# Splitting the second layer's weights in a background stream during the first layer of a two-layer mixer trunk

## The chip, the cores and the metric

The kernel runs on one core of one Trainium2 chip. The metric is the device time of one execution in microseconds. Before the change it is 2655.73 us, the median of 3 runs (2654.89 to 2658.55).

## The reference

A sequence of 2048 tokens of width 1024 passes through two layers. Each layer normalises and modulates its input, projects it once to all heads, runs gated linear attention on one half and differential softmax attention on the other, gates both, and projects back. All inputs are 32-bit floats.

```python
for l in range(DEPTH):                                   # 2 layers
    shift, scale, gate = jnp.split(c_act @ w_ada[l] + b_ada[l], 3, axis=-1)
    h = rms_norm(x, norm_g[l]) * (1.0 + scale[:, None]) + shift[:, None]
    gq, gk, gv, glr, gz, dq, dk, dv, dz = split_columns(h @ w_in[l])
    gqkv = jax.nn.silu(causal_depthwise_conv(jnp.concatenate([gq, gk, gv], axis=-1), conv_w[l]))
    o_gla = gla_branch(*split3(gqkv), glr, gz, w_gk[l], b_gk[l], gla_norm_g[l])
    o_diff = diff_branch(dq, dk, dv, dz, qn_g[l], kn_g[l], lam, lam_init, diff_norm_g[l])
    x = x + gate[:, None] * (jnp.concatenate([o_gla, o_diff], axis=-1) @ w_out[l])
```

## The kernel before, in words

Each layer works through the sequence in four blocks of 512 tokens (`u` = 0 to 3). The dense projections are made of three matmuls for each product: the activations and the weights are each split into a high part of a shorter format and a low part (the rest), and high x high, high x low and low x high are added up. A weight matrix is nine items: four attention heads (items 0 to 3), two pieces of the convolved group (4 and 5), the gate (6) and the two halves of the output projection (7 and 8). Each item has eight weight tiles, one for each 128 rows, so a layer has 72. A tile `w` holds both parts, 128 x 2 x 512, and feeds 12 matmuls of 128x512.

`weights` (L552) delivers such a tile. In a layer's first block (`u` = 0) it loads the raw weights into a tile `raw` (three buffers), casts them to the high part on ScalarE, subtracts on GpSimd for the low part, and writes the tile to DRAM (`wd`). In the three later blocks it reads the kept tile back from `wd`. The tiles `w` come from the pool `p_w` with four buffers (L301).

`dense_gen` (L1013) runs the projections of a block, `out_gen` (L1064) its output projection. `head_evac` (L836) takes a head's result out of PSUM: ScalarE copies queries and keys into a tile `rw` of 128x256 (four buffers), squares are summed, GpSimd takes the power, and VectorE writes the normalised values to a tile `qk`, which TensorE then transposes. `conv_evac` (L674) does the convolution: ScalarE copies a bank into `ub`, VectorE runs four taps into a tile `t` and makes `uT`, with a tanh on ScalarE between. `prep_gen` (L605) makes the input of the next block. The attention writes scores and probabilities in tiles `s`, their transposes in `aT`.

The order of the instructions is decided in two steps. `run_streams` (L518) steps through generators (dense, attention, linear attention, preparation and others), each of which yields estimates of TensorE time or names an event it needs, and records their operations in one list. `Program.order` (L188) then schedules that list: with an estimated duration for each operation it fills each engine, and where several operations are ready on an engine the one recorded first goes first. Buffers of a pool are handed out in the order of recording, so an operation that needs a buffer also waits for the turn of those recorded ahead of it. Each engine and the DMA queue of SyncE (SP) then run their instructions strictly in that order. Every operation is issued from line 284, so all profile rows carry L284 and are told apart by tile names.

Of the kernel before, what the change touches and what calls it, by code (L numbers as in the profile page):

```python
# [11 lines left out]
F32 = mybir.dt.float32  # L12
# [8 lines left out]
P = 128  # L21
D = 1024
KT = D // P
# [264 lines left out]
def trunk_kernel(ctx, tc, x, c, w_ada, b_ada, norm_g, w_in, conv_w, w_gk, b_gk, gla_norm_g,  # L288
# [9 lines left out]
    p_h = pool("p_h", 1)  # L298
    p_x = pool("p_x", 1)
    p_raw = pool("p_raw", 3)  # L300
    p_w = pool("p_w", 4)  # L301
    p_oT = pool("p_oT", 8)
    p_s = pool("p_s", 4)
    p_at = pool("p_at", 3)
# [204 lines left out]
    def done(*ev):  # L509
        events[ev] = clock[0]  # L510

    def need(*ev, lag=0.0):
        return ("need", ev, lag)

    def pe(cost, wait=0.0):
        return ("pe", cost, wait)
# [35 lines left out]
    def weights(l, u, item, k, src, n=None):  # L552
        w = p_w.tile([P, 2, 512], F32R, tag="w", name="w")
        hi, lo = w[:, 0, :], w[:, 1, :]
        kept = WD[l][item][k]
        if u > 0:
            SY.dma_start(w.bitcast(F32), kept)
            return hi, lo
        raw = p_raw.tile([P, 512], F32, tag="raw", name="raw")
        SY.dma_start(raw if n is None else raw.rearrange("p (g n) -> p g n", n=n), src)  # L560
        A.copy(hi, raw)
        G.tensor_tensor(lo, raw, hi.bitcast(F32), op=ALU.subtract)
        if NU > 1:
            SY.dma_start(kept, w.bitcast(F32))
        return hi, lo

    def silu2(dst, ps, shape=(P, 512)):
        th = t2(shape)
# [267 lines left out]
    def head_evac(l, u, hd, banks):  # L836
        key = l * NU + u
        ss = p_sm.tile([P, TT, 4], F32, tag="qss", name="qss", bufs=2)
        rq = p_sm.tile([P, TT, 4], F32, tag="rq", name="rq", bufs=2)
        sz = p_z.tile([P, TT, P], F32, tag="z", name="z")  # L840
        Vt = p_kv.tile([P, TT, P], F32, tag="V", name="Vt")
        qk = []
        for t in range(TT):
            rw = p_t.tile([P, 256], F32, tag="rw", name="rw", bufs=4)
            A.copy(rw, banks[t][:, 0:256])
            th = p_t.tile([P, P], F32, tag="th", name="th", bufs=2)
            A.activation(th, banks[t][:, 384:512], AF.Tanh, scale=0.5)
            V.scalar_tensor_tensor(sz[:, t, :], th, 1.0, banks[t][:, 384:512], op0=ALU.add, op1=ALU.mult)
            A.copy(Vt[:, t, :], banks[t][:, 256:384])
            sq = p_t.tile([P, 256], F32, tag="sq", name="sq", bufs=2)  # L850
            A.activation(sq, rw, AF.Square)
            V.tensor_reduce(ss[:, t, :], sq.rearrange("p (a n) -> p a n", a=4), axis=AX.X, op=ALU.add)
            V.tensor_scalar(ss[:, t, :], ss[:, t, :], 1.0 / 64, EPS, op0=ALU.mult, op1=ALU.add)
            G.tensor_tensor(rq[:, t, :], ss[:, t, :], mhalf[:, 0:4], op=ALU.pow)
            n = p_q.tile([P, 256], F32, tag="qk", name="qk", bufs=4)
            V.tensor_tensor(n.rearrange("p (a n) -> p a n", a=4), rw.rearrange("p (a n) -> p a n", a=4),
                            rq[:, t, :].unsqueeze(2).to_broadcast([P, 4, 64]), op=ALU.mult)
            qk.append(n)
        HD[key, hd] = (qk, Vt, sz)

    def qk_gen(l, u, hd):
# [150 lines left out]

    def dense_gen(l, u, items):  # L1013
        key = l * NU + u
        yield need("h", key, lag=2.0)
        def gla_proj(grp):
            banks = []
            yield from proj_T(l, u, 4 + grp, C_GQ + 512 * grp, banks)
            if grp == 0:
                yield need("gate", key)  # L1020
            else:
                yield need("ktr", key)
            GL[f"cv{grp}"] = conv_evac(l, u, grp, banks)
            done("conv", key, grp)

        def head_proj(hd):
            def ld(k):
                src = w_in[l, k * P:(k + 1) * P, C_D:C_D + 2048].rearrange("p (g n) -> p g n", n=512)
                return weights(l, u, hd, k, src[:, :, hd * P:hd * P + P], n=P)

            banks = []
            yield from proj_N(ld, banks)
            if hd == LAST:
                done("free_h", key + 1)
            if hd >= 1:
                yield need("qkT", key, hd - 1)
            if hd >= 2:
                yield need("attn", key, hd - 2)
            head_evac(l, u, hd, banks)
            done("hev", key, hd)  # L1040

        def gate_proj():
            banks = []
            yield from proj_N(lambda k: weights(l, u, 6, k, w_in[l, k * P:(k + 1) * P, C_GZ:C_GZ + 512]), banks)
            if LAST == 4:
                done("free_h", key + 1)
            yield need("scan", key)
            osb = GL["osb"]
            for t in range(TT):
                sz = t2()  # L1050
                silu2(sz, banks[t])
                G.tensor_tensor(osb[:, t, :], osb[:, t, :], sz, op=ALU.mult)
            done("gz", key)

        LAST = 4
        for it in items:
            if it < 4:
                yield from head_proj(it)
            elif it < 6:
                yield from gla_proj(it - 4)  # L1060
            else:
                yield from gate_proj()
# [43 lines left out]
    def attn_stream():  # L1106
        for l in range(L):
            for u in range(NU):
                for hd in range(4):
                    yield from attn_gen(l, u, hd)  # L1110

    def qk_stream():
        for l in range(L):
            for u in range(NU):
                for hd in range(4):
                    yield from qk_gen(l, u, hd)

    def gla_stream():
        for l in range(L):
            for u in range(NU):  # L1120
                yield from gla_gen(l, u)

    def prep_stream():
        for l in range(L):
            for u in range(NU):
                if l > 0:
                    yield need("x", (l - 1) * NU + u)
                if l or u:
                    yield from prep_gen(l, u, io(l)[0])

    def dense_stream():
# [8 lines left out]
                prev = (l, u)  # L1140
        yield from out_gen(*prev)

    def ada_stream():
        yield need("h", 0)
        yield need("conv", 0, 1)
        yield from ada_part(0, 2, 0.0)
        for l in range(1, L):
            yield need("h", (l - 1) * NU + max(NU - 3, 0))
            yield from ada_part(l, 0, 4.0)
            yield from ada_part(l, 1, 4.0)  # L1150
            yield need("gate", l * NU - 1)
            gate_weights(l)
            yield need("x", l * NU - 1)
            yield from ada_part(l, 2, 1.0)
# [3 lines left out]
    small_vectors(False)  # L1158
    more_vectors()
    gate_weights(0)  # L1160
    run_streams([qk_stream(), attn_stream(), gla_stream(), prep_stream(), ada_stream(), dense_stream()])
    with tc.manual_schedule():
        prog.issue()

# [24 lines left out]
```

## Time and profile before

| | |
|---|---|
| Median of the runs | 2655.73 us (2654.89 to 2658.55) |
| Profiled execution | 2658.48 us |
| Its span | 2656.8 us |
| Mean granted clock of TensorE | 0.995 |
| DMA, mean over the span | 179 GB/s, 476.12 MB |

Durations in the prediction come from the profiled execution. The view by stages gives, for each stretch, the busy time of TensorE, its weight load, VectorE, ScalarE and GpSimd with the number of instructions, then the granted clock, the mean busy share of the 16 DMA engines and GB/s. The first layer's four blocks end at about 345, 655, 985 and 1362 us, and the second layer's first at about 1660 us. Rows of waits read: who waited, in front of the arrow, and for whom, behind it, then us in total, times and the longest.

### The profile page before, as it was taken

What the parts mean: (1) busy time and instruction counts of PE and PEld (TensorE: products, weight loads), DVE (VectorE), ACT (ScalarE), POOL (GpSimd) and SP (SyncE); (2) the same over time, 40 slices, a digit from 0 to 9 for tenths busy, and PEclk for the clock granted to TensorE, in tenths of its full rate; (3) what the DMA queues carried; (4) which work ended last, traced back from release to release, by engine and by line L of the source; (5) the groups of instructions that cost most, each with busy time, mean ns of one, the idle gap of its engine ahead of it and who ended that gap; (6) DMA issues with size and microseconds to landing.
All of it is one profiled execution on the core that took longest, in us unless ns stands there. A gap on an engine that the chain in (4) does not pass through costs nothing. (4 is left out here: it accounts for less than half of the span.)

```text
span 2656.8 us, 41105 instructions
## 1 busy us (share of the span) xinstructions
PE 2563.9 (97%) x13987; PEld 2066.8 (78%) x13987; DVE 1767.1 (67%) x5104; ACT 1206.7 (45%) x2592; POOL 626.2 (24%) x852
## 2 busy tenths in 40 slices
PE   7999899999999999999999989999999999999997
PEld 4777678877888778888777767887788877888886
DVE  4778757874767837776838764667637786387764
ACT  3555524443344533444734563344614456154442
POOL 2455411131010210102144554111121111210111
PEclk9999999999999999999999999999999999999999
DMA  8676586446552455433277756453374433734242
GB/s 281 237 233 238 202 296 202 155 153 216 177 184 98 151 203 175 139 131 133 87 257 254 234 203 241 166 176 135 127 265 147 154 128 116 265 124 150 92 139 103
DMA packets 201612, 476.12 MB, mean 179 GB/s; under 512 B 20734, under 2 KB 78268, under 8 KB 201404
## 3 DMA queue, kind: packets, MB, share of 16 engines
q1 hardware_dynamic: 201404, 473.50, 52.1%
q8 instruction: 111, 1.82, 0.3%
q14 instruction: 97, 0.79, 0.1%
HBM read 362.29 MB, written 111.15 MB: 178 GB/s over the span
## 5 line engine op out<-in xcount | busy, mean ns | idle before, releaser
L284 PE MATMUL acc<-w,hhi 128*128 128x512 f32 x2560 | 842.1, 404 | 6.5 <-DMA w<-wd 2.8
L284 PEld LDWEIGHTS acc<-w,hhi 128*128 128x128 f32 x2560 | 462.3, 189 | 106.0 <-issue 13.2
L284 PE MATMUL acc<-w,hlo 128*128 128x512 f32 x1280 | 506.3, 397 | 0.0
L284 ACT ACTIVATE s<-s,mx 128x512 f32<-128x512 f32 (+15 forms) x256 | 308.1, 1204 | 339.6 <-DVE s L284 337.9
L284 PE MATMUL acc<-hhi,w 128*128 128x512 f32 x1024 | 370.5, 403 | 1.2 <-DVE z L284 0.5
L284 PE MATMUL acc<-w,oh 128*128 128x512 f32 x1024 | 333.8, 401 | 8.9 <-DVE t L284 5.0
L284 DVE TENSOR_SCALAR_CACHE_REDUCE s<-sc,mx 64x64 f32<-64x64 f32 (+5 forms) x640 | 307.4, 485 | 42.9 <-PE sc L284 24.7
L284 PEld LDWEIGHTS acc<-w,hlo 128*128 128x128 f32 x1280 | 241.2, 188 | 49.9 <-issue 2.0
L284 POOL MEMSET s<- 64x64 f32 x256 | 39.3, 155 | 1020.6 <-DVE s L284 466.2
L284 POOL TENSOR_TENSOR w<-raw,w 128x512 fp32r<-128x512 f32 x144 | 195.1, 1365 | 198.2 <-ACT w L284 152.7
L284 PEld LDWEIGHTS acc<-w,oh 128*128 128x128 f32 x1024 | 189.9, 189 | 54.4 <-DVE t L284 9.4
L284 PEld LDWEIGHTS acc<-hhi,w 128*128 128x128 f32 x1024 | 192.3, 188 | 39.3 <-issue 1.2
L284 ACT COPY aT<-tp 128x512 f32<-128x512 f32 (+2 forms) x320 | 162.7, 521 | 114.4 <-PE tp L284 110.6
L284 PE MATMUL po<-Vj,aT 128*128 128x128 f32 x1536 | 205.4, 278 | 5.1 <-ACT aT L284 4.8
L284 PE MATMUL acc<-w,ol 128*128 128x512 f32 x512 | 202.7, 400 | 1.0 <-DVE ol L284 0.7
L284 PEld LDWEIGHTS po<-Vj,aT 128*128 128x128 f32 x1536 | 191.7, 193 | 14.8 <-ACT aT L284 9.5
L284 DVE SCALAR_TENSOR_TENSOR s<-s,r 128x512 f32<-128x512 f32 (+2 forms) x320 | 200.5, 676 | 2.9
L284 DVE TENSOR_SCALAR_CACHE_REDUCE s<-sc 128x512 f32<-128x512 f32 (+4 forms) x256 | 158.5, 623 | 65.2 <-PE sc L284 61.1
L284 PE MATMUL acc<-hlo,w 128*128 128x512 f32 x512 | 201.2, 393 | 0.0
L284 DVE TENSOR_TENSOR ol<-oT,oh 128x512 fp32r<-128x512 f32 x128 | 105.6, 832 | 119.1 <-ACT oh L284 108.0
L284 PE MATMUL tp<-ident,s 128*128 128x128 f32 x1088 | 172.2, 274 | 11.8 <-DVE s L284 9.4
L284 POOL TENSOR_TENSOR rq<-qss,mhalf 128x4 f32<-128x4 f32 x128 | 129.0, 1027 | 191.4 <-DVE qss L284 191.0
(167 smaller groups left out, 4204.4 us busy)
## 6 DMA issues: line engine op xcount, KB each, us to landing
w<-wd SPq DMA_DIRECT2D x432, 512.0 KB, 3.7
wd<-w SPq DMA_DIRECT2D x144, 512.0 KB, 3.2
raw<-in_w_in_dram SPq DMA_DIRECT2D x112, 256.0 KB, 4.0
Kj<-kd SPq DMA_DIRECT2D x48, 512.0 KB, 4.9
wr<-in_w_ada_dram SPq DMA_DIRECT2D x128, 128.0 KB, 2.8
kd<-Kt SPq DMA_DIRECT2D x24, 512.0 KB, 3.0
Vj<-vd SPq DMA_DIRECT2D x48, 256.0 KB, 4.1
xt<-in_x_dram SPq DMA_DIRECT2D x16, 512.0 KB, 4.0
```

What stands on the lines that cost most here:

```text
L284: getattr(self.engines[e], method)(*[real(a) for a in args], **{k: real(v) for k, v in kw.items()})
```

## The change

The first block of the second layer no longer splits its weights. A new stream, `split_stream`, does it during the first layer: after an event of the first block (`conv`, 0, 1) it takes the items 0, 4, 1, 5, 2, 3, 6, 7, 8 of the second layer and calls `split_ahead` for each, which loads, casts, subtracts and writes the same tiles as `weights` did. Between two tiles it lets 12.5 us of estimated TensorE time pass. In the second layer every block reads the kept tiles, and its first block needs the nine `split` events first. The pool `p_w` has five buffers instead of four. `head_evac` normalises `rw` in place, and the tile `qk` (four buffers of 128x256) is gone.

```diff
-    p_w = pool("p_w", 4)
+    p_w = pool("p_w", 5)
...
         kept = WD[l][item][k]
-        if u > 0:
+        if u + l > 0:
             SY.dma_start(w.bitcast(F32), kept)
             return hi, lo
...
+    def source(l, item, k):
+        rows = slice(k * P, (k + 1) * P)
+        if item < 4:
+            return w_in[l, rows, C_D:C_D + 2048].rearrange("p (g n) -> p g n", n=512)[:, :, item * P:item * P + P]
+        if item < 7:
+            col = (C_GQ, C_GQ + 512, C_GZ)[item - 4]
+            return w_in[l, rows, col:col + 512]
+        return w_out[l, rows, 512 * (item - 7):512 * (item - 6)]
+
+    def split_ahead(l, item):
+        for k in range(KT):
+            w = p_w.tile([P, 2, 512], F32R, tag="w", name="w")
+            raw = p_raw.tile([P, 512], F32, tag="raw", name="raw")
+            SY.dma_start(raw if item >= 4 else raw.rearrange("p (g n) -> p g n", n=P), source(l, item, k))
+            A.copy(w[:, 0, :], raw)
+            G.tensor_tensor(w[:, 1, :], raw, w[:, 0, :].bitcast(F32), op=ALU.subtract)
+            SY.dma_start(WD[l][item][k], w.bitcast(F32))
+            yield pe(0, 12.5)
+        done("split", l, item)
...
-            n = p_q.tile([P, 256], F32, tag="qk", name="qk", bufs=4)
-            V.tensor_tensor(n.rearrange("p (a n) -> p a n", a=4), rw.rearrange("p (a n) -> p a n", a=4),
-                            rq[:, t, :].unsqueeze(2).to_broadcast([P, 4, 64]), op=ALU.mult)
-            qk.append(n)
+            rv = rw.rearrange("p (a n) -> p a n", a=4)
+            V.tensor_tensor(rv, rv, rq[:, t, :].unsqueeze(2).to_broadcast([P, 4, 64]), op=ALU.mult)
+            qk.append(rw)
...
+        for item in range(9):
+            if l and not u:
+                yield need("split", l, item)
         yield need("h", key, lag=2.0)
...
+    def split_stream():
+        for l in range(1, L):
+            yield need("conv", (l - 1) * NU, 1)
+            for item in (0, 4, 1, 5, 2, 3, 6, 7, 8):
+                yield from split_ahead(l, item)
...
-    run_streams([qk_stream(), attn_stream(), gla_stream(), prep_stream(), ada_stream(), dense_stream()])
+    run_streams([qk_stream(), attn_stream(), gla_stream(), prep_stream(), ada_stream(), split_stream(),
+                 dense_stream()])
```

The change puts the casts and writes into other places of the order. Counted between the ends of the output projections, the 72 splits of the second layer stand in the first layer's four blocks with 14, 23, 25 and 10. The rows that follow are instructions in their order, with buffer numbers in the names.

The first place is ScalarE in layer 0's second block, in the convolution. First before, then with the change.

```order
L284 COPY aT_4358<-tp_4332 128x256
L284 ACTIVATE junk_4375,oss_4376<-po_4335 128x128
L284 ACTIVATE t2_4399<-t2_4338 128x512
L284 COPY ub_4402<-acc_4023 128x512
L284 ACTIVATE t2_4439<-t2_4397 128x512
L284 ACTIVATE s_4250,ls_4463<-s_4250,mx_4425 128x1024
```
```order
L284 ACTIVATE junk_4478,oss_4479<-po_4447 128x128
L284 ACTIVATE t2_4514<-t2_4463 128x512
L284 COPY ub_4517<-acc_4119 128x512
L284 CAST w_4543<-raw_4159 128x512
L284 ACTIVATE t2_4554<-t2_4511 128x512
L284 ACTIVATE s_4377,ls_4594<-s_4377,mx_4540 128x1024
```

A cast of a second-layer weight now stands between the last copy out of PSUM and the tanh (`t2`) and exponential (`s`) behind it.

The second place is ScalarE in layer 1's first block, behind the first head's copies. First before, then with the change.

```order
L284 ACTIVATE sq_14345<-rw_14333 128x256
L284 CAST w_14352<-raw_14249 128x512
L284 CAST w_14358<-raw_14275 128x512
L284 CAST w_14374<-raw_14307 128x512
L284 ACTIVATE qh_14407<-tp_14399,G1_599 64x512 x2
L284 CAST w_14433<-raw_14391 128x512
L284 CAST Kt_14439<-tp_14426 64x512 x2
L284 CAST w_14457<-raw_14404 128x512
L284 ACTIVATE s_13670,ls_14472<-s_13670,mx_14460 128x128
```
```order
L284 ACTIVATE sq_14734<-rw_14723 128x256
L284 ACTIVATE qh_14780<-tp_14774,G1_599 64x512 x2
L284 CAST Kt_14804<-tp_14797 64x512 x2
L284 ACTIVATE s_14106,ls_14835<-s_14106,mx_14826 128x128
L284 ACTIVATE s_14258,ls_14835<-s_14258,mx_14837 128x128
```

The five weight casts between the head's copies, the query and key casts (`qh`, `Kt`) and the first exponentials are gone.

The third place is the DMA queue of SP in layer 0's second block, around the write of that block's first keys (`kd1_0`). First before, then with the change.

```order
L284 DMA kd1_0_4121<-Kt_4098 128x1024
L284 DMA wr_4127<-in_w_ada_dram 128x256
L284 DMA wr_4131<-in_w_ada_dram 128x256
L284 DMA w_4152<-wd0_1_0_1074 128x1024
L284 DMA w_4199<-wd0_1_1_1108 128x1024
```
```order
L284 DMA kd1_0_4217<-Kt_4196 128x1024
L284 DMA wr_4224<-in_w_ada_dram 128x256
L284 DMA wr_4229<-in_w_ada_dram 128x256
L284 DMA wd1_1_1_4234<-w_4212 128x1024
L284 DMA raw_4240<-in_w_in_dram 128x4x128
L284 DMA w_4245<-wd0_1_1_1104 128x1024
```

A split's write (`wd1_1_1`, of the second layer) and the next raw load now stand in front of the weight load that follows.

## The prediction

> **What bounds the kernel now.** I read the page's busy totals first, then the span cut into stages.
>
> ```profile
> span 2656.8 us, 41105 instructions
> PE 2563.9 (97%) x13987; PEld 2066.8 (78%) x13987; DVE 1767.1 (67%) x5104; ACT 1206.7 (45%) x2592; POOL 626.2 (24%) x852
> ```
>
> TensorE (PE) is busy for 2563.9 of 2656.8 us, so only 92.9 us of the span can be won without removing matmuls, and the change removes none. The question is therefore in which stage PE stands idle. The next view gives the busy time of PE, weight load, VectorE (DVE), ScalarE (ACT) and GpSimd (POOL) by stage, then the granted PE clock, the DMA share and GB/s. I cut at the ends of the output projections. The rows are the eight blocks of 512 tokens, four per layer, with a start, a joint and a tail.
>
> ```profile
> 60.00:345.00 285.00, 262.03 (x1314) 197.93 (x1312) 212.72 (x547) 150.81 (x356) 141.46 (x152) 0.99 0.69 235
> 345.00:655.00 310.00, 302.64 (x1634) 244.53 (x1635) 211.29 (x636) 129.77 (x297) 57.12 (x91) 1.00 0.58 195
> 655.00:985.00 330.00, 328.70 (x1843) 270.39 (x1842) 221.17 (x654) 151.14 (x313) 52.28 (x88) 1.00 0.47 161
> 985.00:1320.00 335.00, 332.88 (x1897) 273.56 (x1896) 237.65 (x705) 161.85 (x307) 45.72 (x77) 1.00 0.41 140
> ...
> 1362.00:1660.00 298.00, 280.60 (x1405) 219.38 (x1404) 190.38 (x514) 145.37 (x350) 151.71 (x161) 0.99 0.70 241
> 1660.00:1950.00 290.00, 284.39 (x1529) 228.08 (x1528) 183.55 (x569) 129.75 (x297) 48.24 (x84) 1.00 0.46 161
> ```
>
> Length minus PE busy is PE's idle time. It is 22.97 us in the first block of layer 0 and 17.40 us in the first block of layer 1. In the other rows it is 7.36, 1.30 and 2.12 us (layer 0, blocks 1 to 3) and 5.61 us (layer 1, block 1). So the two blocks that split weights idle most. They are also the ones at clock 0.99, and 1% of 298 us is another 3.0 us. The most that can come back in layer 1's first block is 17.4 + 3.0 = 20.4 us, or 0.77% of the span.
>
> What PE waits for in that block (us in total, times, longest):
>
> ```profile
> PE tp L284 <- DVE uT L284: 3.3, 2, 2.5
> PE tp L284 <- DVE s L284: 3.1, 5, 1.7
> PE sc L284 <- DVE xss L284: 3.0, 1, 3.0
> PE sc L284 <- DVE Kt L284: 1.8, 3, 0.8
> PE acc L284 <- DVE t L284: 1.7, 1, 1.7
> PE po L284 <- ACT aT L284: 1.3, 2, 1.0
> ```
>
> None of these is a weight tile, and the rows left out are 1.0 us or less and on DVE or ACT too. PE does not wait for the split itself. It waits for the convolution, softmax and normalising chains on DVE and ACT. The split can only matter through what it does to those two queues, and that makes the gain hard to size.
>
> **The change part by part.** The rows of the split in that block come first, then what ACT waits for there.
>
> ```profile
> L284 ACT CAST w<-raw x69: 602/620/723, 1363.7 to 1637.7; 128x512 fp32r<-128x512 f32 x69
> L284 POOL TENSOR_TENSOR w<-raw,w x69: 1266/1292/1892, 1366.8 to 1638.4; 128x512 fp32r<-128x512 f32 x69
> ```
> ```profile
> ACT w L284 <- DMA raw<-in_w_in_dram: 23.5, 13, 3.8
> ACT w L284 <- PE acc L284: 21.8, 13, 4.9
> ```
>
> *Removed from layer 1's first block.* 69 casts x 0.620 = 42.8 us leave ACT, of its 145.4. 69 subtracts x 1.292 = 89.1 us leave POOL, of 151.7. ACT also stands 23.5 + 21.8 = 45.3 us at the head of its queue with a cast that waits for its raw tile or for a free weight tile. Behind that cast stand the exponentials, the tanh of the convolution and the PSUM copies, as the rows of the order show. The subtracts on POOL also hold DVE up, as the same DVE instruction shows in this block and in layer 0's second block, which has no split (min/median/max ns):
>
> ```profile
> L284 DVE SCALAR_TENSOR_TENSOR t<-ub,vec,t x24: 737/744/1661, 1415.3 to 1490.3; 128x512 f32<-128x512 f32 x24
> ```
> ```profile
> L284 DVE SCALAR_TENSOR_TENSOR t<-ub,vec,t x24: 733/746/754, 400.4 to 519.8; 128x512 f32<-128x512 f32 x24
> ```
>
> The median is the same but the longest is 1661 against 754 ns, so single DVE steps of the convolution lose up to 0.91 us, and the wait that costs PE most in all (uT) is for the end of that convolution. The idle time of 17.4 us can stay whole (gain 0), or it can fall to the 5.61 us of the next block, which loads its weights ready (gain 11.8). The first block has the least attention work to put between dependent steps, so I do not take the whole fall. I take half of 17.4, a **gain of 8.7 us**.
>
> *The clock.* These rows are PE around its uT wait.
>
> ```profile
> 1428.19 0.39 PE L284 MATMUL acc<-w,hlo 128*128 128x512 f32 x1
> 1428.42 0.39 PE L284 MATMUL acc<-w,hhi 128*128 128x512 f32 x1
> 1431.30 1.09 PE L284 MATMUL tp<-ident,uT 128*128 128x128 f32 x4 [2.49 <-DVE uT L284]
> 1432.04 0.78 PE L284 MATMUL acc<-w,hhi 128*128 128x512 f32 x1
> ...
> 1433.90 0.63 PE L284 MATMUL acc<-w,hlo 128*128 128x512 f32 x1
> 1434.32 0.73 PE L284 MATMUL acc<-w,hhi 128*128 128x512 f32 x2
> ```
>
> Before the wait large matmuls start 0.23 us apart. After it they start 0.42 us apart until about 1434.3. A wait of 2.5 us thus costs some 1.5 us more. I return half of the block's 3.0 us with half of the waits, a **gain of 1.5** (bounds 0 and 3.0). [...]
>
> *Added to layer 0.* The order of the changed kernel has 14 splits in its first block and 23, 25 and 10 in the next three. Each brings a raw load, a cast, a subtract and a write to DRAM. Layer 1's first block reads 72 tiles of 512 KB back instead of loading raw ones. Price of a split in a first block, from the idle and clock that I ascribe to it above the level of the next block: (17.4 - 5.6 + 3.0) / 69 = 0.21 us. The 14 in layer 0's first block, where ACT (150.8 us) and POOL (141.5) already carry 72, cost 14 x 0.21 = **3.0 us** (bounds 0 and double, 6.0).
>
> The other 58 go into blocks where PE has attention work to cover with. In the two later rows, idle is only 1.30 and 2.12 us of 330 and 335. The trace has no split beside such work. The bounds are 0 and 58 x 0.21 = 12.2 us. I take a quarter, since those rows are nearest to no loss, which is **3.0 us**. The cover is the matmul queue of PE, and where it fails the full 0.21 is paid. The 58 x 0.620 = 36 us of casts go to ACT, which is busy 129.8 to 161.9 us per block there.
>
> *The fifth weight tile.* Issue and landing:
>
> ```profile
> w<-wd SPq DMA_DIRECT2D x432, 512.0 KB, 3.7
> wd<-w SPq DMA_DIRECT2D x144, 512.0 KB, 3.2
> raw<-in_w_in_dram SPq DMA_DIRECT2D x112, 256.0 KB, 4.0
> ```
>
> A weight tile feeds 12 matmuls, 12 x 0.23 = 2.8 us of PE. With four tiles a load can start three tiles (8.3 us) ahead of its use, and with five it is four (11.0 us). A split tile occupies one slot for its cast, subtract and write, at least 0.62 + 1.29 + 3.2 = 5.1 us. While it does, the stream falls back to the four of before, whose 8.3 us still covers 3.7. So I expect no new weight wait. PE's only weight wait between 345 and 1320 us is this one:
>
> ```profile
> PE acc L284 <- DMA w<-wd: 2.8, 2, 1.7
> ```
>
> It lies right behind the first block. I count a **gain of 2.0** (bounds 0 and 2.8). Split writes also stand in SP's in-order queue, waiting for POOL, with weight loads behind them. That wait is inside the same 8.3 us.
>
> *In place normalising of rw.* The multiply keeps its size and engine, so it costs 0. The cover is that the next head's copies into rw come at least one projection later, 96 matmuls or 22 us, and the transposes that free rw are done by then. If that cover went, the copy would hold PSUM banks and each microsecond would be PE's.
>
> **Sum.** -8.7 - 1.5 + 3.0 + 3.0 - 2.0 = -6.2 us. The profiled execution took 2658.48 us, of which 1.7 lie outside the span, so it becomes 2652.3. The median of the runs, 2655.73, is 2.75 us below the profiled one, which gives **2649.5 us**. Its own range is 2642 to 2654.
>
> **Rivals.**
>
> *Nothing comes back.* PE's waits are the depth of short chains in a block with little attention, not crowding. The waits for xss (3.0) and Kt speak for this, the ACT queue's 45.3 us against. Then the first block returns 3.0 with its clock, the fifth tile 1.0, layer 0 pays 4.0, and the time stays at 2655.7.
>
> *Casts hold ACT's queue in layer 0 (slower).* In the second to fourth blocks a cast that waits for a weight tile stands in front of an exponential, the exponential in front of the DVE sum, and that in front of PE's transposes. The 45.3 us of waiting over 69 casts are 0.66 us per cast. If half reaches PE, 58 x 0.33 = 19 us come in place of my 3.0, and the net is +9.9, or 2665.6. It makes the kernel slower by over 0.2% from (6.2 + 3.0 + 5.3) / 58 = 0.25 us per split on. Against it speak the idle times of 1.30 and 2.12 us, although ACT waits for PE in those blocks too.
>
> *Subtracts lock DVE in layer 0.* If one in three of the 58 subtracts costs PE the 0.91 us of the convolution row, that is 17.6 in place of 3.0, or 2664.1. [...] DVE is not the bound in those blocks, at 67 to 71% of each.
>
> That the splits would not move at all is excluded by the counts in the order.
>
> **How the numbers follow.** My forecast gets 0.55, nothing comes back 0.27, the ACT queue 0.13, the lock 0.05. From the unknown terms the lowest time is 2655.7 - 11.8 - 3.0 - 2.8 = 2638.1. Upwards the range takes in the lock's 2664. What lies beyond, most of the ACT rival and the all-bad sum (+18.2), is under 2 in 10. About 0.2% (5.3 us) is what a measurement of this kernel can tell from no change. The forecast lies only just beyond it, so of its 0.55 I count 0.48 as faster and 0.07 as the same. Of the second case's 0.27, 0.23 stay the same and 0.02 fall to either side. Of the slower rivals' 0.18, 0.16 are slower and 0.02 the same. That makes 0.50 faster, 0.32 the same, 0.18 slower.
>
> **What would show it.** Right: PE's idle time in layer 1's first block falls from 17.4 to about 9, uT and s waits halve, ACT has no cast there, the longest convolution step is near 754 ns, and idle time in layer 0's blocks 1 to 3 grows by some 3 us from 10.8. Wrong: idle time there grows by over 10 us with waits for s, aT or t behind casts, new waits for w<-wd appear, or the first block keeps its idle time.

## The result, and the profile after

The changed kernel takes 2674.16 us (median of 6 runs, 2673.18 to 2679.27) against 2656.53 us before (6 runs, 2654.89 to 2661.27). The ratio is 1.0068, with an interval of 1.0055 to 1.0081: it is **slower by 0.7%**, where 2649.5 us was forecast. Its profiled execution took 2673.8 us. The page of the changed kernel begins:

```profile
span 2672.1 us, 41217 instructions
PE 2571.7 (96%) x13987; PEld 2071.5 (78%) x13987; DVE 1763.7 (66%) x5104; ACT 1207.7 (45%) x2592; POOL 626.6 (23%) x852
```

PE has the same 13987 matmuls, and yet is busy 7.8 us longer. So PE does not only wait more, some of its matmuls also take longer. The cut into stages tells where. These are the rows of the changed kernel, cut at the exact ends of layer 0's four blocks and of layer 1's first (busy time of PE, PEld, DVE, ACT, POOL; then clock, DMA share, GB/s):

```profile
60.00:350.00 290.00, 262.78 (x1310) 200.24 (x1309) 212.64 (x545) 157.80 (x370) 158.59 (x164) 0.98 0.79 269
350.00:669.00 319.00, 305.14 (x1619) 243.08 (x1618) 216.70 (x637) 142.84 (x320) 85.87 (x111) 0.99 0.71 240
669.00:1010.60 341.60, 334.27 (x1851) 271.48 (x1851) 232.00 (x655) 165.16 (x338) 87.72 (x114) 1.00 0.63 217
1010.60:1391.60 381.00, 373.64 (x2109) 306.85 (x2109) 262.05 (x743) 179.13 (x339) 68.50 (x98) 1.00 0.49 165
1391.60:1661.40 269.80, 263.40 (x1346) 209.27 (x1345) 164.12 (x513) 107.89 (x281) 55.41 (x89) 0.99 0.55 186
```

The same blocks of the kernel before, cut at their own ends:

```profile
60.00:343.60 283.60, 261.43 (x1313) 197.76 (x1312) 211.48 (x545) 150.81 (x356) 140.06 (x151) 0.99 0.69 234
343.60:651.00 307.40, 299.24 (x1620) 241.38 (x1619) 211.16 (x637) 129.77 (x297) 54.52 (x89) 1.00 0.58 196
651.00:982.90 331.90, 330.60 (x1851) 271.99 (x1850) 221.11 (x655) 151.14 (x313) 54.19 (x89) 1.00 0.48 162
982.90:1361.30 378.40, 372.95 (x2109) 307.12 (x2108) 259.04 (x743) 174.97 (x332) 59.07 (x91) 1.00 0.42 144
1361.30:1645.40 284.10, 266.71 (x1345) 208.20 (x1344) 189.61 (x513) 145.37 (x350) 147.32 (x158) 0.99 0.69 237
```

Layer 1's first block falls from 284.1 to 269.8 us, a gain of 14.3. Layer 0's four blocks grow by 6.4, 11.6, 9.7 and 2.6 us, **30.3 us in all**. The balance is +16.0, and the span grew by 15.3. So the weights are split ahead and layer 1 does get faster. Layer 0 pays twice as much as layer 1 gains.

What PE still waits for in layer 1's first block of the changed kernel:

```profile
PE sc L284 <- DVE xss L284: 3.0, 1, 3.0
PE sc L284 <- DVE Kt L284: 1.6, 3, 0.5
PE acc L284 <- DVE t L284: 1.3, 2, 0.7
```

The waits for uT (3.3) and s (3.1) are gone. Those for xss and Kt are as they were. The longest convolution step there, min/median/max:

```profile
L284 DVE SCALAR_TENSOR_TENSOR t<-ub,vec,t x24: 730/744/752, 1443.9 to 1509.7; 128x512 f32<-128x512 f32 x24
```

It was 1661 ns, and the lock has left this block. In layer 0 behind its first block the same row has a longest step of 754 ns in the kernel before and 1772 in the changed kernel. First before, then changed:

```profile
L284 DVE SCALAR_TENSOR_TENSOR t<-ub,vec,t x72: 725/746/754, 400.4 to 1169.3; 128x512 f32<-128x512 f32 x72
```

```profile
L284 DVE SCALAR_TENSOR_TENSOR t<-ub,vec,t x72: 723/746/1772, 410.9 to 1200.0; 128x512 f32<-128x512 f32 x72
```

In the same stretch, the largest waits of PE in the changed kernel, then those for `s` in the kernel before, then what SP's DMA queue waits for in the changed kernel:

```profile
PE acc L284 <- DMA w<-wd: 5.6, 6, 3.4
PE tp L284 <- DVE z L284: 3.3, 4, 1.2
PE sc L284 <- DVE s L284: 2.9, 5, 0.7
PE tp L284 <- DVE s L284: 2.9, 7, 0.7
```
```profile
PE tp L284 <- DVE s L284: 1.5, 5, 0.4
PE sc L284 <- DVE s L284: 1.2, 3, 0.6
```
```profile
SPq L284 <- PE acc L284: 308.7, 105, 15.1
SPq L284 <- POOL w L284: 170.7, 44, 11.4
SPq L284 <- DMA wd<-w: 61.2, 34, 4.4
```

SP's second row was 4.0 us before, and its third is new. SP stands 170.7 us with a write that waits for the subtract. It stands 61.2 us with a weight load whose tile a split's write has not yet left. The weight waits that the prediction excluded are there (5.6 us, six times, against 2.8 us, twice, before). They are not the larger part. If all of PE's waits in the three blocks are sorted by who ended them, those for DVE grow from 8.4 to 16.7 us, those for ACT from 3.0 to 5.2, and those for DMAs from 2.8 to 5.8. The longest weight wait, in PE's order of time:

```profile
355.90 0.62 PE L284 MATMUL acc<-w,hhi 128*128 128x512 f32 x2
356.35 0.39 PE L284 MATMUL acc<-w,hlo 128*128 128x512 f32 x1
360.09 1.22 PE L284 MATMUL acc<-w,hhi 128*128 128x512 f32 x2 [3.36 <-DMA w<-wd]
361.11 0.63 PE L284 MATMUL acc<-w,hlo 128*128 128x512 f32 x1
361.54 1.05 PE L284 MATMUL acc<-w,hhi 128*128 128x512 f32 x2
...
365.38 1.01 PE L284 MATMUL acc<-w,hhi 128*128 128x512 f32 x2
366.23 0.40 PE L284 MATMUL acc<-w,hlo 128*128 128x512 f32 x1
```

After the stall three matmuls take 1.45 us (360.09 to 361.54) instead of 3 x 0.23. The 6.1 us from 360.09 to 366.23 hold 14 matmuls, which at 0.23 us would take 3.2. So a wait of 3.4 us cost another 2.9. Such stretches count as busy (PE 6.11 of the 6.80 us from 359.4 to 366.2): in blocks 1 to 3, 13.6 of the 23.9 us are idle time and 10.3 are added PE busy time. The clock is only a part of the 10.3. In these blocks the trace grants half the clock for 10.2 us, against 3.4 us before, and 6.8 us more at half speed are worth some 3.4 us. What makes the rest of the 10.3 is not shown.

### The profile page after: what moved, and what is told of

It reads as the page before. It is cut to its first block, busy times and chain, and to the rows that moved or that the text cites. A ratio compares the mean times of both kernels' runs of the same rounds, so it can differ in the third digit from the quotient of the medians.

```text
span 2672.1 us, 41217 instructions
## 1 busy us (share of the span) xinstructions
PE 2571.7 (96%) x13987; PEld 2071.5 (78%) x13987; DVE 1763.7 (66%) x5104; ACT 1207.7 (45%) x2592; POOL 626.6 (23%) x852
## 5 line engine op out<-in xcount | busy, mean ns | idle before, releaser
L284 PEld LDWEIGHTS acc<-w,hhi 128*128 128x128 f32 x2560 | 463.2, 189 | 111.9 <-issue 12.2
L284 PE MATMUL acc<-w,oh 128*128 128x512 f32 x1024 | 335.3, 404 | 13.9 <-DVE t L284 6.6
L284 PEld LDWEIGHTS po<-Vj,aT 128*128 128x128 f32 x1536 | 191.4, 193 | 17.2 <-ACT aT L284 11.0
```

The lines of the kernel that those rows point to most:

```text
L284: getattr(self.engines[e], method)(*[real(a) for a in args], **{k: real(v) for k, v in kw.items()})
```

## The experiments

Every difference below is a ratio to the kernel before on the same chip, with its 95% interval; 0.1% is 2.7 us. "Price" is the ratio less that of the kernel without any split (none), times 2656 us. By the intervals a price is good to about 5 us. Block lengths are of one profiled execution each: none and turn_only, which take the same time, differ by 3.5 us in block 1, so block differences of that size are uncertain. The last column of the table is layer 1's first block.

| kernel | ratio | price, us | L0: 0 | 1 | 2 | 3 | L1: 0 |
|---|---|---|---|---|---|---|---|
| before | 1 | 12.2 | 343.6 | 307.4 | 331.9 | 378.4 | 284.1 |
| the change | 1.0068 | 30.3 | 350.0 | 319.0 | 341.6 | 381.0 | 269.8 |
| none | 0.9954 [0.9939, 0.9969] | 0 | 340.5 | 309.5 | 332.1 | 378.8 | 272.1 |
| turn_only | 0.9956 [0.9939, 0.9972] | 0.5 | 339.1 | 306.0 | 331.9 | 378.5 | 270.7 |
| cast_only | 0.9950 [0.9936, 0.9965] | -1.1 | 344.3 | 306.2 | 332.2 | 376.9 | 270.0 |
| sub_only | 0.9999 [0.9990, 1.0009] | 12.0 | 347.9 | 309.0 | 336.4 | 380.8 | 269.0 |
| compute_only | 1.0024 [1.0014, 1.0034] | 18.6 | 349.0 | 312.9 | 337.4 | 379.1 | 269.2 |
| dma_turn | 1.0005 [0.9996, 1.0015] | 13.5 | 355.5 | 308.1 | 332.7 | 379.2 | 269.8 |
| dma_only | 1.0057 [1.0042, 1.0072] | 27.4 | 349.2 | 315.7 | 343.1 | 379.2 | 273.5 |
| own_slot | 1.0091 [1.0074, 1.0107] | 36.4 | 347.4 | 324.3 | 340.4 | 379.3 | 270.8 |
| lowprio | 1.0078 [1.0063, 1.0093] | 32.9 | 349.5 | 327.2 | 339.6 | 377.7 | 270.6 |
| sub_dve | 1.0056 [1.0041, 1.0071] | 27.1 | 351.6 | 317.0 | 337.8 | 383.0 | 268.7 |
| act_write | 1.0206 [1.0191, 1.0221] | 66.9 | 354.4 | 335.3 | 350.4 | 389.3 | 271.7 |
| late | 1.0065 [1.0050, 1.0080] | 29.5 | 341.4 | 319.4 | 343.8 | 384.2 | 269.0 |
| late_dve | 1.0038 [1.0027, 1.0049] | 22.3 | 341.6 | 315.5 | 342.4 | 381.8 | 269.4 |
| turn_own | 1.0082 [1.0064, 1.0100] | 34.0 | 349.3 | 318.1 | 342.4 | 382.6 | 271.6 |
| turn_own_late_dve | 1.0019 [1.0010, 1.0029] | 17.3 | 342.7 | 311.6 | 338.5 | 380.2 | 274.3 |

The theory at the start was that the cast holds ACT's queue, since a split takes turns among the shared weight tiles. Its rivals were the lock on DVE and the DMAs with SP's queue.

### What all of it costs, and its halves

**none.**

```diff
-        kept = WD[l][item][k]
+        kept = WD[0][item][k]
...
         for k in range(KT):
-            w = p_w.tile([P, 2, 512], F32R, tag="w", name="w")
...
-            SY.dma_start(WD[l][item][k], w.bitcast(F32))
             yield pe(0, 12.5)
```

> The changed kernel without any split of the second layer: the stream only lets its estimated time pass, and the second layer reads the first layer's kept weights (its own weights are left out). By the blocks' ends the splits cost the first layer 30 us and gave 14 back in the second. All theories: the first layer's blocks 1 to 3 are again within 2 us of before (307, 332, 378 us), the second layer's first block stays near 270 us, in all some 2641 us. If the fifth weight tile or the normalising in place were what costs, the time would stay above 2656.

Measured: 2642.67 us. As far as these kernels tell, this is the ceiling of splitting ahead: with 72 splits for nothing the kernel gains 12.2 us. The splits cost 12.2 us where they stood and 30.3 us where they were put. The fifth tile and the `rw` edit are in this kernel too, and layer 0's blocks sum to 1360.9 us against 1361.3 before, so neither gave anything that these profiles can tell. The weight wait (2.8) is gone here, and PE waits for t instead, 3.6 us where it was 1.4:

```profile
PE acc L284 <- DVE t L284: 3.6, 4, 2.2
```

**dma_only.**

```diff
-            raw = p_raw.tile([P, 512], F32, tag="raw", name="raw")
-            SY.dma_start(raw if item >= 4 else raw.rearrange(...), source(l, item, k))
-            A.copy(w[:, 0, :], raw)
-            G.tensor_tensor(w[:, 1, :], raw, w[:, 0, :].bitcast(F32), op=ALU.subtract)
-            SY.dma_start(WD[l][item][k], w.bitcast(F32))
+            hi = w[:, 0, :].bitcast(F32)
+            SY.dma_start(hi if item >= 4 else hi.rearrange(...), source(l, item, k))
+            SY.dma_start(WD[l][item][k][:, 0, :], w[:, 0, :].bitcast(F32))
+            SY.dma_start(WD[l][item][k][:, 1, :], w[:, 0, :].bitcast(F32))
```

> As without any split, but the stream keeps its DMAs (raw load of 256 KB into the weight tile, two writes of 256 KB) and its turn of a weight tile; cast and subtract are left out, and the second layer reads the first layer's weights. Theory DMA traffic: most of the 30 us is there, 2664 us or more. Theory ACT's queue and theory lock on DVE: near the kernel without any split, under 2647 us.

**compute_only.**

```diff
-            SY.dma_start(raw if item >= 4 else raw.rearrange(...), source(l, item, k))
-            A.copy(w[:, 0, :], raw)
-            G.tensor_tensor(w[:, 1, :], raw, w[:, 0, :].bitcast(F32), op=ALU.subtract)
-            SY.dma_start(WD[l][item][k], w.bitcast(F32))
+            A.copy(w[:, 0, :], fix)    # fix: a constant tile, shaped to 128x512
+            G.tensor_tensor(w[:, 1, :], fix, w[:, 0, :].bitcast(F32), op=ALU.subtract)
```

> As without any split, but the stream keeps cast and subtract (from a constant) and its turn of a weight tile; its DMAs are left out, and the second layer reads the first layer's weights. Theories ACT's queue and lock on DVE: most of the 30 us is there, 2664 us or more. Theory DMA traffic: under 2647 us.

Measured: 2671.80 us for the DMAs with a held weight tile and no arithmetic, 2662.62 us for the arithmetic without DMAs. Both halves cost, 27.4 and 18.6 us, and they sum to more than the 30.3 of the whole. Each was forecast to cost next to nothing if the other's theory held, so no single theory holds, and the causes overlap.

### The theory of the ACT queue

**own_slot** gives the splits a tile of their own, **lowprio** besides takes their operations last among those that are ready.

```diff
-    p_w = pool("p_w", 5)
+    p_w = pool("p_w", 4)
+    p_ws = pool("p_ws", 1)
...
-            w = p_w.tile([P, 2, 512], F32R, tag="w", name="w")
+            w = p_ws.tile([P, 2, 512], F32R, tag="ws", name="ws")
```

> The changed kernel with four weight tiles for the projections and one of its own for the splits, the same SBUF in all; nothing is left out. Theory ACT's queue (a cast waits there for its turn of a shared weight tile): most of the first layer's 30 us goes, about 2648 us. Theories lock on DVE and DMA traffic: within 4 us of the changed kernel, 2674 us.

> The changed kernel with a tile of its own for the splits, and a scheduler that takes an operation of the split stream only when nothing else is ready on its engine; nothing is left out. Theory order (splits recorded early go ahead of later work on ScalarE, GpSimd and the DMA queue): the first layer's loss of 30 us falls to under 15, about 2660 us or less. Theory lock on VectorE and theory DMA traffic: within 5 us of 2676.

The edit of lowprio beside that:

```diff
-                heapq.heappush(avail[e], heapq.heappop(pend[e])[1])
-            i = heapq.heappop(avail[e])
+                i = heapq.heappop(pend[e])[1]
+                heapq.heappush(avail[e], (ops[i][7], i))    # ops[i][7]: 1 for a split's operation
+            i = heapq.heappop(avail[e])[1]
```

Measured: 2678.28 and 2679.19 us. Neither helps, and block 1 gets worse (324.3 and 327.2). One thing had moved: without the turns of the shared tiles the order puts 39 splits into block 1 (23 in the change). So they speak against the theory without settling it. The same trap spoiled three further kernels, in which one part of a split used a tile of its own or none.

**cast_own, sub_own, dma_own.** In each, `split_ahead` keeps one part: the cast, the subtract, or the raw load with two writes straight from `raw`.

```diff
+            w = p_ws.tile([P, 2, 512], F32R, tag="ws", name="ws")
+            A.copy(w[:, 0, :], fix)                                          # cast_own
...
+            G.tensor_tensor(w[:, 1, :], fix, fix, op=ALU.subtract)           # sub_own
...
+            SY.dma_start(WD[l][item][k][:, 0, :], raw)                       # dma_own
+            SY.dma_start(WD[l][item][k][:, 1, :], raw)
```

> As the kernel without any split (2642.7 us), but the stream does the 72 casts on ScalarE, from a constant and into a tile of its own, so that no cast waits for a weight tile; subtract and DMAs are left out, and the second layer reads the first layer's weights. Theory ScalarE time (the cast itself delays exponentials): 2652 us or more. Theory lock on VectorE by the subtract, theory turns of the weight tiles, theory DMA: within 4 us of 2643.

> As the kernel without any split, but the stream does the 72 subtracts on GpSimd, from constants and into a tile of its own; cast and DMAs are left out, and the second layer reads the first layer's weights. Theory lock on VectorE: 2652 us or more, with longer single VectorE steps in the first layer's blocks 1 to 3. All others: within 4 us of 2643.

> As the kernel without any split, but the stream does the raw loads (256 KB) into raw tiles and writes each back twice (2 x 256 KB), with no weight tile and no work on any engine; the second layer reads the first layer's weights. Theory DMA traffic: the whole excess of the run with a weight tile (29 us) stays, 2665 us or more, with waits for weight loads. Theory turns of the weight tiles: within 6 us of 2643.

Measured: 2647.12 us (0.9957 [0.9942, 0.9972]), 2664.41 us (1.0030 [1.0019, 1.0040]) and 2675.05 us (1.0065 [1.0048, 1.0083]). With nothing to wait for, all 72 casts and all 72 subtracts moved into layer 0's first block. The DMAs of 14 splits went into that block and 58 into the next. So they do not test the change's places. What they do show: 72 casts more in layer 0's first block cost nothing that can be measured (a price of 0.8 us); 72 subtracts there lengthen it to 364.8 us. And with the DMAs of 58 splits in it, and no weight tile held, block 1 takes 327.0 us at a DMA share of 0.91, 17.5 us more than in none, where the share is 0.59. The page of dma_own shows four slices in a row, from 334 to 602 us, at 90% or more and 320 to 372 GB/s.

**turn_only and cast_only** keep the change's places. A split takes its turn of a shared tile, and writes four columns or a whole cast into it.

```diff
+            A.copy(w[:, 0, 0:4], ident[:, 0:4])     # turn_only
...
+            A.copy(w[:, 0, :], fix)                 # cast_only
```

> The stream takes its turn of a shared weight tile, as in the change (14, 23, 25 and 10 in the first layer's blocks), with a cast of 4 columns from a constant as the only work; the second layer reads the first layer's weights. Compared with the kernel without any split (2642.7 us) and with cast and subtract in the same places (2662.6). Theory turns (an in-order wait of ScalarE for a weight tile): most of the 20 us, 2655 us or more. Theory lock: within 4 us of 2643.

> As with turns alone, but with the whole cast of 512 columns on ScalarE; subtract and DMAs left out. The kernel with casts in a tile of their own did not test this, since its 72 casts all fell into the first block. Theory ScalarE (turns or time): most of the 20 us, 2655 us or more. Theory lock: within 5 us of 2643.

Measured: 2643.88 and 2643.63 us, prices of 0.5 and -1.1 us. **The theory of the ACT queue falls.** In cast_only, in layer 0 behind its first block, ACT waits like this:

```profile
ACT w L284 <- PE acc L284: 116.8, 33, 14.0
```

It stands 116.8 us at the head of its queue with casts whose tile PE has not yet left, and the kernel's time does not show it. In both kernels the source is a constant, so a cast here never waits for a DMA.

### The lock

**sub_only** keeps the turns and the places, and of the split only the subtract.

```diff
+            G.tensor_tensor(w[:, 1, :], fix, fix, op=ALU.subtract)
```

> As with turns alone, but with the subtract on GpSimd from constants in the place of the cast, in the same blocks; no cast and no DMAs. Theory lock on VectorE: most of the 20 us, 2655 us or more, and single VectorE steps near 1.7 us. Theory ScalarE: within 5 us of 2643.

Measured: 2655.87 us, a price of 12.0 us. The convolution steps in layer 0 behind its first block, in sub_only:

```profile
L284 DVE SCALAR_TENSOR_TENSOR t<-ub,vec,t x72: 724/747/1450, 403.7 to 1180.9; 128x512 f32<-128x512 f32 x72
```

The blocks of sub_only, in the columns of the stages:

```profile
347.90:656.90 309.00, 301.44 (x1619) 241.19 (x1618) 215.49 (x636) 129.25 (x297) 80.49 (x112) 1.00 0.58 191
656.90:993.30 336.40, 333.02 (x1851) 271.62 (x1851) 227.17 (x655) 151.06 (x313) 80.30 (x114) 1.00 0.48 160
993.30:1374.10 380.80, 374.08 (x2110) 308.27 (x2109) 261.06 (x743) 173.33 (x329) 66.23 (x99) 0.99 0.44 145
```

and the same of none:

```profile
340.50:650.00 309.50, 300.90 (x1619) 242.34 (x1618) 210.75 (x636) 129.81 (x297) 54.93 (x89) 0.99 0.59 191
650.00:982.20 332.20, 330.92 (x1852) 272.08 (x1852) 221.23 (x655) 151.00 (x313) 54.15 (x89) 1.00 0.50 162
982.20:1361.00 378.80, 373.36 (x2110) 307.97 (x2109) 258.22 (x744) 173.30 (x329) 55.46 (x89) 0.99 0.44 144
```

DVE does the same work and is busy 4.7, 5.9 and 2.8 us longer, 13.5 us for the 58 subtracts. Nothing else was added, so POOL's subtracts hold DVE up, by 0.23 us each on average. POOL's own work is not late: DVE waits 21.4 us for POOL's results in those blocks, and 24.3 in none. The three blocks grow by 5.7 us together (2.3 of it idle time of PE), the first one by 7.4. By which waits the lock reaches PE is thus shown only in part. The longest convolution step here exceeds its median by 0.70 us (1450 against 747 ns); the median is that of before (746 ns), so most of these steps are not held up.

This run also bears on SP's queue. In the same three blocks SP stands behind these subtracts as long as in the change, with weight loads that need the split's tile, and yet PE waits for no weight there:

```profile
SPq L284 <- POOL w L284: 193.5, 46, 12.8
```

**sub_dve** is the whole change with the subtract on VectorE.

```diff
-            G.tensor_tensor(w[:, 1, :], raw, w[:, 0, :].bitcast(F32), op=ALU.subtract)
+            V.tensor_tensor(w[:, 1, :], raw, w[:, 0, :].bitcast(F32), op=ALU.subtract)
```

> The whole change, nothing left out, with the split's subtract on VectorE instead of GpSimd (0.83 us each by the same operation on ol), in the same blocks 14, 23, 25, 10. Theory lock (a GpSimd subtract blocks a VectorE step that PE waits for): 8 to 14 us less than the change, 2660 to 2666. If VectorE's time counts and not the lock: 2674 or more.

Measured: 2672.55 us, 3 us better by the ratios, within the intervals, and not the 8 to 14 us of the theory. The lock is gone, as the convolution steps of this kernel show:

```profile
L284 DVE SCALAR_TENSOR_TENSOR t<-ub,vec,t x72: 725/747/754, 415.5 to 1196.4; 128x512 f32<-128x512 f32 x72
```

PE's waits for DVE behind the first block fall from 16.7 to 9.1 us, near the 8.4 of before. But its weight waits there have doubled:

```profile
PE acc L284 <- DMA w<-wd: 11.9, 7, 2.6
```

What the one gave back, the other took. Why the weight waits grow is not shown.

### The DMAs and SP's queue

**dma_turn** has the DMAs of the change in its places, but holds no weight tile over them.

```diff
-            A.copy(w[:, 0, :], raw)
-            G.tensor_tensor(w[:, 1, :], raw, w[:, 0, :].bitcast(F32), op=ALU.subtract)
-            SY.dma_start(WD[l][item][k], w.bitcast(F32))
+            A.copy(w[:, 0, 0:4], raw[:, 0:4])
+            SY.dma_start(WD[l][item][k][:, 0, :], raw)
+            SY.dma_start(WD[l][item][k][:, 1, :], raw)
```

> As with turns alone, but with the raw load (256 KB) and two writes of 256 KB from the raw tile, which no weight tile is held for; no subtract, and a cast of 4 columns. The run with DMAs alone held a weight tile from the raw load to the write, which the change does not. Theory DMA traffic: 2655 us or more, with PE waiting for w<-wd. Theory that the held weight tile made that run slow: within 6 us of the run with turns alone.

Measured: 2658.79 us, a price of 13.5 us, and all of it in the first block (355.5 against 340.5). The time fits the traffic theory, but the waits for w<-wd that it named do not come: behind the first block PE has none. Part of that is this kernel's own: it holds the three raw tiles until its writes land, and PE in the first block waits for layer 0's own casts:

```profile
PE acc L284 <- ACT w L284: 6.2, 5, 4.2
```

Its blocks 1 and 2 by stages:

```profile
355.50:663.60 308.10, 301.27 (x1619) 242.31 (x1618) 209.47 (x634) 131.63 (x320) 54.29 (x89) 1.00 0.75 254
663.60:996.30 332.70, 330.94 (x1851) 271.92 (x1850) 220.93 (x655) 154.90 (x338) 54.03 (x89) 1.00 0.66 220
```

They take 308.1 and 332.7 us, against 309.5 and 332.2 in the rows of none, though the DMA share is 0.75 and 0.66 instead of 0.59 and 0.50. **At that density the traffic by itself, with its writes in SP's queue, costs nothing there that these profiles can tell.** Packed closer it does, as dma_own's block 1 shows (17.5 us more at a share of 0.91). dma_only moves the same bytes and holds the weight tile from the raw load until its writes have landed. Its blocks 1 and 2 take 315.7 and 343.1 us, and PE waits there:

```profile
PE acc L284 <- DMA w<-wd: 11.3, 5, 5.4
```

So the next theory was the held tile: five buffers and in-order use of them, of which a split keeps one until its write lands.

**act_write** moves the split's write from SP's queue to ScalarE's.

```diff
-            SY.dma_start(WD[l][item][k], w.bitcast(F32))
+            A.dma_start(WD[l][item][k], w.bitcast(F32))
```

> The whole change, nothing left out, with the split's write issued by ScalarE instead of SP, so that no weight load stands behind a write that waits for GpSimd. Theory queue (the loads behind the write come late, w<-wd 5.6 us of PE waits in blocks 1 to 3): 6 us or more less than the change, 2668 or below. Theory traffic: within 4 us of 2674.

Measured: 2713.31 us, the slowest of all; every block of layer 0 is longer. ACT now issues the write in its own order, behind the subtract. That this wait is what costs is not shown: ACT's idle time right in front of the 58 writes in blocks 1 to 3 is 29.0 us in all and 3.1 at the longest. The run says nothing for SP's queue.

**late and late_dve** begin the splits after layer 0's first block (none there, 22, 28 and 22 in the next), late_dve with the subtract on VectorE.

```diff
-            yield pe(0, 12.5)
+            yield pe(0, 11.0)
...
-            yield need("conv", (l - 1) * NU, 1)
+            yield need("conv", (l - 1) * NU + 1, 0)
```

> The whole change, nothing left out, with the stream beginning in the first layer's second block and a tile each 11 us of estimated time: 0, 22, 28 and 22 splits in the four blocks. By the runs without DMAs or without cast and subtract, a split costs most in the first block (0.7 us each). So some 6 us less than the change, about 2668. If the price is the same in each block: 2674.

> Both, begin in the second block and subtract on VectorE, nothing left out. If the two gains add: about 2656 to 2660, level with the kernel before. If both only move the same waits: as the better of the two.

Measured: 2675.34 and 2667.13 us. The first block is back at 341.4 and 341.6. In late the other blocks lose most of what it gained, and the time is the change's: the later start moves the price and does not lower it. late_dve is 5 us better than sub_dve by the ratios, within the intervals, and its forecast of 2656 to 2660 is missed.

**turn_own and turn_own_late_dve** test the held tile. The split takes a turn of a shared tile for a copy of four columns, so it keeps its place, and does its work in a tile of its own.

```diff
+            A.copy(w[:, 0, 0:4], raw[:, 0:4])
+            w = p_ws.tile([P, 2, 512], F32R, tag="ws", name="ws")
             A.copy(w[:, 0, :], raw)
```

> The whole change, nothing left out, but the cast, the subtract and the write use a split tile of their own; of the shared weight tiles (four now, so that the memory is the same) each split only takes one turn, for a copy of four columns on ScalarE. So no shared tile is held until a write lands, and the splits stand at nearly the same places as in the change (13, 26, 25 and 8 by block). Theory of the held tile: TensorE's waits for w<-wd in layer 0's blocks 1 to 3 go from 5.6 us to near none, those blocks fall by some 10 us, and the time is near 2664 or less. Rival (the traffic and SP's in-order queue alone make that part): the blocks stay, and the time is within 4 us of the change's 2674.

> As turn_own, and the splits start only after layer 0's first block (0, 24, 28 and 20 by block), and the subtract is on VectorE. If the price of the first block, the lock of VectorE by GpSimd's subtracts and the held tile are the three causes and add up, the time is 2650 to 2656, at or below before. If the held tile is no cause, it is near late_dve, 2667.

Measured: 2678.23 and 2662.56 us. The first is a miss: blocks 1 and 2 stay at 318.1 and 342.4. The weight waits are 5.0 us, of which 4.8 are one wait at the start of block 1, so inside the blocks they are gone, as the theory said, and it bought nothing. But the one split tile brings ACT new waits, in layer 0 behind its first block:

```profile
ACT ws L284 <- DMA raw<-in_w_in_dram: 36.4, 13, 7.9
ACT ws L284 <- DMA wd<-ws: 24.6, 7, 8.8
ACT ws L284 <- DMA raw<-in_w_out_dram: 14.8, 5, 6.1
```

The second lies between its two forecasts, and fits the theory in part. Against late_dve, whose weight waits are these,

```profile
PE acc L284 <- DMA w<-wd: 11.8, 7, 3.5
```

it has

```profile
PE acc L284 <- DMA w<-wd: 2.6, 2, 1.7
```

and blocks 1 to 3 fall by 9.4 us, the time by 5 us by the ratios, whose intervals just overlap. So the hold makes the weight waits inside the blocks, and they cost time where the lock is gone. With the lock in place, taking the hold away for ACT's new waits bought nothing. Even with all three removed (the first block, the lock, the hold) 72 splits cost 17.3 us, more than the 12.2 in their old place. **No full version here beats the kernel before.**

What stays open is the rest of blocks 1 and 2 in the change and in turn_own. The casts alone, the subtracts alone and the DMAs alone change those two blocks by -3.2, +3.8 and -0.8 us together, cast and subtract chained (compute_only) by +8.7, the DMAs that hold a weight tile (dma_only) by +17.2, and the whole change by +19.0. That points to the hold and to the chain, in which load, cast, subtract and write each wait at the head of an in-order queue, but for the change and turn_own it is argued and not shown. The ACT waits of turn_own for DMAs would fit; a cast that waits only for a DMA was not tried by itself.

## Why the prediction was wrong, point by point

- **Layer 1's first block: right in kind, too small.** Forecast was 8.7 us of waits and 1.5 of clock; measured are 11.0 us of idle time (17.4 to 6.4) and 3.3 us of PE busy. The idle time fell nearly to the next block's level (a gain of 11.8), where half of the 17.4 was taken. The signs named came true: uT and s waits gone, no cast on ACT, longest step 752 ns. "Nothing comes back" is refuted. Which of the two, ACT's queue or the lock, gave this gain no run separates, since every one takes both out of this block. The clock term is not borne out: the trace grants half the clock for 6.8 us of this block in either kernel, so the 3.3 us are something else, and that they cover the 1.5 is luck.
- **Layer 0's first block: too small.** 14 splits were to cost 3.0 us (0 to 6.0); the block grew by 6.4.
- **The 58 other splits: this step failed.** "The other 58 go into blocks where PE has attention work to cover with. [...] I take a quarter." It gave 3.0 us, 12.2 at the worst; measured are 23.9, or 0.41 us per split. The 0.21 us itself was near for the old place, where 72 splits cost 12.2 us, or 0.17 each. Idle times of 1.3 and 2.1 us were read as room for more work. They say that PE never waits, not how much later its suppliers may be. DVE is busy 216.7 of 319 and 232.0 of 341.6 us, and PE's waits for its results doubled. The price also held little for matmuls that get slower (3.0 of 14.8 us, as clock), when added PE busy time is 10.3 of the 23.9.
- **The fifth tile: failed.** "So I expect no new weight wait" counted a gain of 2.0. The kernel none has the fifth tile and no gain, and in the full change there are six weight waits. The slot, reckoned at 5.1 us, is about 6 by an estimate: 2.0 us in the median from the cast's start to the write's issue, and some 4 until the write lands (4.0 in the median, `wd<-w` behind the first block of the change). The 8.3 us of lead counted the load from an idle queue. "That wait is inside the same 8.3 us" did not hold for SP's queue, which stands up to 11.4 us with a write in front of loads. The write is late because the subtract in front of it waits at the head of POOL's queue for its cast, in layer 0 behind the first block of the change:

```profile
POOL w L284 <- ACT w L284: 226.6, 42, 24.1
```

  That SP stands is not enough for a weight wait, as sub_only shows (12.8 us at the longest, none). By dma_only against dma_turn and late_dve against turn_own_late_dve, what makes the waits is the tile held until the write has landed.
- **`rw` in place: right as far as it was tested**, since none loses nothing by it.
- **The rivals.** The ACT queue (0.13) gave a nearer time, 2665.6, for a wrong reason: cast_only and turn_only cost nothing. The lock (0.05) was real. It was forecast at 17.6 us for the 58 subtracts and measures 12.0 for all 72 by itself, more than half in the first block. Held weight tiles were no rival of their own, though the prediction's own sign for being wrong named new waits for w<-wd. It treated causes as alternatives; here they stood side by side.

## What to carry to other kernels

Work moved out of a crowded stage is paid for where it lands: measure first what the stage gives with the work left out (12.2 us here) and what the work costs at its new place (30.3 us), since only the difference is won. Low idle time of the bounding engine was no free room here (1.3 and 2.1 us in two blocks that then grew by 9.7 and 2.6 us); ask which shared buffer the moved work holds, until when, and which in-order queue stands behind it. When one part is taken away to find the cause, look first whether the others kept their places, as several kernels here tested something else than was meant.

## What the runs showed of the hardware that was not expected

- POOL's 128x512 subtracts, alone, made DVE 13.5 us busier over 58 of them with unchanged DVE work, 0.23 us each, the longest single step growing from 754 (before) to 1450 ns. With operands from DMA and cast (the change) the longest is 1772 ns.
- A weight wait of 3.36 us was followed by 6.1 us of matmuls at about half speed, which cost 2.9 us more. The granted clock was 0.50 from 359.4 to 366.2 us.
- DMA shares of 0.75 and 0.66 instead of 0.59 and 0.50 cost no time that the profiles can tell in two blocks in which PE is busy over 97% (dma_turn). With the same bytes and a weight tile held over them the two blocks took 658.8 us instead of 640.8 (dma_only), and at a share of 0.91 without such a tile one block took 17.5 us more (dma_own).
